# A gate one load later, a copied operand with a place of its own, and a free PSUM bank taken first, in a two-matmul GELU kernel

## The chip, the cores and the metric

The kernel runs on 1 core of one Trainium2 chip. The metric is device time of one execution in microseconds (us); the profile's span is some 1.8 us shorter, because it runs from the first to the last instruction. Most executions agree within 0.3%. Every verdict uses fast runs alone. A ratio is the mean time of one kernel's fast runs over that of the other's of the same rounds, so it is not quite the ratio of the medians quoted beside it. Profiles are one execution each, which will matter below.

## The reference, cut to what matters

```python
m, k, n, p = 1024, 1024, 2048, 1024          # a: m x k, b: k x n, c: n x p, all float32
h = np.matmul(a, b)
h = 0.5 * h * (1 + np.tanh(np.sqrt(2 / np.pi) * (h + 0.044715 * h ** 3)))
return np.matmul(h, c).astype(np.float32)
```

## The kernel before

Both matmuls use a Winograd-like scheme: seven products of quarter matrices instead of eight, paid for with sums of operands on VectorE (`s1` to `s4`, `t1` to `t4`) and with copies on ScalarE (`plain_s`, `plain_t`). The scheme runs three times: `zero` and `one` are parts of the first matmul, `two` is the second.

Twelve plain loads of 512 KB bring `a` and a quarter of `b` as float32. Fourteen casting loads, issued by GpSimd, bring the rest as bf16. A tiny GpSimd copy, the gate, keeps the casting loads back: it reads one element of a plain load, so it waits for that load, and the casting loads stand behind it in GpSimd's queue.

```python
    load_a(0, 0); load_b(0); load_a(1, 0)              # (the kernel has one call a line)
    for q in range(1, 4):
        load_a(0, q)                                   # q = 3: the tenth load
        load_b(q)                                      #        the eleventh
        load_a(1, q)                                   #        the twelfth
    nc.gpsimd.tensor_copy(gate, sta[1][:, 0, 1, 3, 0:1])   # waits for the tenth
    ...
    for _ in range(7):                                 # TensorE warm-up
        nc.tensor.matmul(wps, warm[:, 0:128], warm, start=True, stop=True)
    for k in range(0, KT, 4):                          # the first two casting loads
        nc.gpsimd.dma_start(out=b1[:, k:k + 4, H:], in_=bv[:, k:k + 4, ds(H, H)])
    ...
    def stir(n):                                       # more warm-up, called with 7 and 8
        for _ in range(n):
            nc.tensor.matmul(ps[0, 3][:, 0:128], warm[:, 0:128], warm[:, 0:128],
                             start=True, stop=True, skip_group_check=True)
```

In `one` the operand `s[3]`, a copy that ScalarE makes, shares a buffer (`x01`) with `s[1]`. So it can only be made when product P6 has read `s[1]`, in four pieces during P7. (P1 to P7 are the code's names. In order of running, P5 is the third product, P6 the fourth and P7 the fifth; the "seventh product" of the prediction is P7.)

```python
    one.s = [x31, x01, x21, x01]
    def between1(n):
        ...
        elif n[:2] == "P7":
            one.plain_s(4, int(n[2]))
```

The product loop of `two`, cut. The second product fills PSUM banks 4, 5, 6, which VectorE reads in `plus`; the third product (P5) fills banks 4, 5, 6, 7:

```python
        for j in J if w is not two else range(3):
            p = bank(P2[j])                            # Y = (4, 5, 6, 7)
            w.product(p, A12, B21, j, True)
            done(0, 0, j, plus(p, p1[j]))
        between("P2")
        py = [bank(i) for i in PY]                     # PY = Y as well
        for j in J:
            w.product(py[j], w.s[0], w.t[0], j, True)
```

Of the kernel before, what the change touches and what calls it, by code (L numbers as in the profile page):

```python
# [10 lines left out]
F32R = mybir.dt.float32r  # L11
# [8 lines left out]
def kernel(ctx, tc, a, b, c, out):  # L20
    nc = tc.nc
# [3 lines left out]
    H = 512  # L25
# [14 lines left out]
    def slot(tag, shape, dt, name):  # L40
        return big.tile(shape, dt, name=name, tag=tag)

    def bank(i, shape=(128, H), dt=F32, name="ps"):
        return pp.tile(list(shape), dt, name=name, tag=f"bank{i}", padded_shape=None)

    def pieces(tag, bufs, shape, dt, name):
        return small.tile(shape, dt, name=name, tag=tag, bufs=bufs)
# [5 lines left out]
    gate = consts.tile([128, 1], F32, name="gate")  # L53
# [5 lines left out]
    b1 = slot("b1", [128, KT, 1024], BF16, "b1")  # L59
# [4 lines left out]
    stb = slot("x0", [128, KT, H], F32, "stb")  # L64
    sta = [slot(f"x{i}", [128, 2, 2, 4, 256], F32, "sta") for i in (1, 3)]
# [13 lines left out]
        load_b(q)  # L79
        load_a(1, q)  # L80

    nc.gpsimd.tensor_copy(gate, sta[1][:, 0, 1, 3, 0:1])
    nc.scalar.activation(g, warm[:, 0:1], AF.Gelu_apprx_tanh)
    wps = bank(7, name="warmps")
    for _ in range(7):
# [117 lines left out]
    def quarters(b, c0, w):  # L203
        return [[b[:, 0:4, ds(c0, w)], b[:, 4:8, ds(c0, w)]],
                [b[:, 0:4, ds(c0 + w, w)], b[:, 4:8, ds(c0 + w, w)]]]

    zero = Seven(4, quarters(b1, H, 256), BB, [None] * 4, [None] * 4, 2)
    one = Seven(4, quarters(b2, 0, H), BB, [None] * 4, zero.t)
# [64 lines left out]
    Y = (4, 5, 6, 7)  # L273

    def snap(tag, p, name):
        st = pieces(tag, 4, [128, H], F32, name)
        nc.scalar.activation(st, p, AF.Copy)  # L277
        return st

    def plus(p, st):  # L280
        ot = pieces("o", 4, [128, H], F32, "ot")
        nc.vector.tensor_tensor(out=ot, in0=p, in1=st, op=ADD)  # L282
        return ot

    def seven(w, done, between):

        (A11, A12), (A21, A22) = w.A
        (B11, B12), (B21, B22) = w.B
        J = range(w.n)
        PX = X[:w.n]  # L290
        P2, PY = (X[2:], Y[:2]) if w.n == 2 else (Y, Y)
        px = [bank(i) for i in PX]
        p1, v, u = {}, {}, {}
        for j in J:
            w.product(px[j], A11, B11, j, True)
            if w is two and j == 3:
                p1[j] = pieces("ab", 2, [128, H], F32, "p1")
                nc.scalar.activation(p1[j], px[j], AF.Copy)
            else:
                p1[j] = snap("m", px[j], "p1")  # L300
        between("P1")
        for j in J if w is not two else range(3):
            p = bank(P2[j])
# [3 lines that stand above are left out]
        py = [bank(i) for i in PY]  # L307
        for j in J:
            w.product(py[j], w.s[0], w.t[0], j, True)
        between("P5")  # L310
        for j in J:
            w.product(px[j], w.s[1], w.t[1], j, False)
            v[j] = snap("v", px[j], "v")
        between("P6")
        c22 = []
        for j in J:
            w.product(px[j], w.s[2], w.t[2], j, False)
            u[j] = snap("m", px[j], "u")
            c22.append(plus(py[j], u[j]))
            between(f"P7{j}")  # L320

        def p3(first):
            for j in J:
                if first:
                    done(1, 1, j, c22[j])
                w.product(py[j], w.last_s, w.t[3], j, False)
                done(0, 1, j, plus(py[j], v[j]))
            between("P3")

        def p4(first):  # L330
            for j in J:
                if first:
                    done(1, 1, j, c22[j])
                w.product(px[j], w.s[3], w.last_t, j, False)
                done(1, 0, j, px[j])

        for i, f in enumerate((p4, p3) if w.n == 2 else (p3, p4)):
            f(i == 0)
        if w is two:

            for i in range(2):
                r = ds(i * 256, 256)
                p = bank(Y[i])
                w.product(p, A12, B21, 3, True, i * 256, 256)
                ot = pieces("e", 2, [128, 256], F32, "ot")
                nc.vector.tensor_tensor(out=ot, in0=p[:, r], in1=p1[3][:, r], op=ADD)  # L346
                store(3, i * 256, 256, ot)


    two = Seven(8, [[hT[0][:, 0:8], hT[0][:, 8:16]], [hT[1][:, 0:8], hT[1][:, 8:16]]],  # L350
                [[c_sb[:, 0:8, 0:H], c_sb[:, 0:8, H:]], [c_sb[:, 8:16, 0:H], c_sb[:, 8:16, H:]]],
                [None] * 4, [None] * 4)
# [16 lines left out]
        gelu(8 + 4 * i + j, l, p)  # L369

    def between1(n):
        if n == "P2":
            one.s3()
        elif n == "P5":
            one.s4(one.s[0])
        elif n[:2] == "P7":
            one.plain_s(4, int(n[2]))
        elif n == "P3":
            two.t[0] = slot("x1", [128, 8, H], F32R, "x2")
            two.t1(4)  # L380
            two.s[0] = slot("b2", [128, 8, H], F32R, "s2")
            two.s1(4)
            two.t[1] = slot("x2", [128, 8, H], F32R, "x2")
            two.t2(4)

    zero.s1()
    zero.s2()
    seven(zero, done0, between0)
    one.s1()
    one.s2()  # L390
    seven(one, done1, between1)


# [4 lines left out]
    def store(mt, q0, w, ot, eng=None):  # L398
        (eng or nc.sync).dma_start(out=out[ts(mt, 128), ds(q0, w)], in_=ot)
# [11 lines left out]
    def between2(n):  # L411
# [12 lines left out]
        elif n == "P73":  # L424
            two.t4(two.t[1], 4)

    seven(two, done2, between2)


# [28 lines left out]
```

## Time and profile before

| | before |
|---|---|
| time, median of 4 runs | 121.95 us (121.84 to 122.01) |
| the profiled execution | 122.19 us, span 120.4 us |
| TensorE busy | 112.5 us, 93% of the span |
| VectorE / ScalarE busy | 75% / 48% |

TensorE is the bound, so only its gaps can be won. The lines that show them are in the prediction below. One part of the page I had passed over. It is the list of DMA queues, with packets, MB and the share of sixteen engines' time:

```profile
q0 software_dynamic: 5344, 7.34, 34.9%
q1 hardware_dynamic: 8192, 10.49, 25.5%
q8 instruction: 4, 0.07, 0.2%
q14 instruction: 2, 0.02, 0.0%
```

The first two are the casting and the plain traffic. The `q8` row is four packets of 16 KB, and 0.2% of the DMA time. It turned out to decide the largest term of the prediction.

### The profile page before, as it was taken

To read this page: it belongs to the slowest core of one execution; us is meant where nothing else is said; L and a number is where in the kernel's file an instruction comes from. 1 tells how busy PE (TensorE), PEld (TensorE's weight loads), DVE (VectorE), ACT (ScalarE), POOL (GpSimd) and SP (SyncE) were. 2 spreads that over 40 slices of the span, in tenths; PEclk is the share of its full clock that TensorE was granted. 3 is DMA by queue.
4 is the path that set the end of the run, shared out by engine and by line. 5 is a ranking of instruction groups with operands and counts; after the bars stand their busy time and mean duration, and the time that the engine had idled before them with its cause. 6 is when DMAs were issued, how large, how long until landed. Compare 5 with 4: busy or idle time off the path is not lost.

```text
span 120.4 us, 1483 instructions
## 1 busy us (share of the span) xinstructions
PE 112.5 (93%) x550; PEld 76.0 (63%) x550; DVE 90.1 (75%) x96; ACT 57.9 (48%) x96; POOL 11.0 (9%) x21
## 2 busy tenths in 40 slices
PE   6997999499999999999999999999999999999990
PEld 2644454144677645888887444468888888888860
DVE  0243678389898599970669999999999986964570
ACT  4046343898877584436969736900023893000000
POOL 2000008932242000000000000000000000000000
PEclk9999999999999999999999999999999999999998
DMA  3999999999999999997000000043000002004993
GB/s 97 274 375 361 365 355 275 197 206 207 207 207 211 211 213 212 210 211 148 3 0 0 5 0 0 0 147 115 0 0 0 0 5 87 0 8 181 363 357 137
DMA packets 13542, 17.91 MB, mean 149 GB/s; under 512 B 736, under 2 KB 8928, under 8 KB 13536
## 3 DMA queue, kind: packets, MB, share of 16 engines
q0 software_dynamic: 5344, 7.34, 34.9%
q1 hardware_dynamic: 8192, 10.49, 25.5%
q8 instruction: 4, 0.07, 0.2%
q14 instruction: 2, 0.02, 0.0%
HBM read 20.97 MB, written 4.19 MB: 209 GB/s over the span
## 4 chain that ended last, share of the span: by engine, by line
PE 59%; DVE 10%; SPq 9%; DMA 9%; issue 5%; ACT 5%; ACTq 0%; DVEq 0%
PE ps L193 55%; DMA sta<-in_a_dram 9%; SPq L68 5%; DVE s L151 4%; DVE x L151 4%; SPq L72 4%; PE ps L106 3%; DVE ot L282 2%; ACT u L277 2%; ACT hT L110 1%; ACT x L189 1%; ACT ab L100 1%; PE pt L129 1%; DVE ot L346 0%; ACTq L100 0%
## 5 line engine op out<-in xcount | busy, mean ns | idle before, releaser
L193 PE MATMUL ps<-x,s 128*128 128x512 f32 x128 | 29.5, 390 | 0.1
L193 PEld LDWEIGHTS ps<-x,s 128*128 128x128 f32 x128 | 24.0, 188 | 5.6 <-DVE ot L282 0.6
L193 PE MATMUL ps<-x,x 128*128 128x512 f32 x80 | 19.1, 394 | 0.0
L106 PE MATMUL ps<-aT,b 128*128 128x512 bf16 x64 | 15.9, 379 | 2.4 <-ACT b L135 1.4
L193 PEld LDWEIGHTS ps<-x,x 128*128 128x128 f32 x80 | 15.0, 188 | 3.3
L193 PE MATMUL ps<-x 128*128 128x512 f32 x72 | 16.8, 391 | 0.0
L193 PEld LDWEIGHTS ps<-x 128*128 128x128 f32 x72 | 13.2, 188 | 3.3 <-ACT v L277 0.2
L277 ACT ACTIVATE v<-ps 128x512 f32<-128x512 f32 x10 | 6.0, 598 | 18.3 <-PE ps L193 18.3
L193 PE MATMUL ps<-c_sb,hT 128*128 128x512 bf16 (+1 forms) x72 | 14.2, 355 | 0.2 <-ACT hT L110 0.2
L110 ACT ACTIVATE hT<-ot 128x512 bf16<-128x512 f32 x18 | 10.8, 627 | 4.3 <-DVE ot L282 4.2
L282 DVE TENSOR_TENSOR ot<-ps,v 128x512 f32<-128x512 f32 x10 | 6.7, 688 | 6.7 <-DMA out_dram<-ot 3.9
L106 PEld LDWEIGHTS <-b 128*128 128x128 bf16 x64 | 5.8, 97 | 9.3 <-ACT b L135 2.5
L193 PEld LDWEIGHTS <-hT 128*128 128x128 bf16 x72 | 7.0, 98 | 7.3 <-issue 0.8
L130 DVE COPY aT<-pt 128x1024 bf16<-128x1024 bf16 x8 | 5.5, 692 | 7.3 <-PE pt L129 7.3
L282 DVE TENSOR_TENSOR ot<-ps,u 128x512 f32<-128x512 f32 x10 | 6.8, 691 | 5.7 <-ACT u L277 5.7
L193 PE MATMUL ps<-aT,b 128*128 128x512 bf16 x48 | 10.7, 379 | 0.0
L151 DVE TENSOR_TENSOR x<-c_sb 128x1024 fp32r<-128x1024 bf16 x8 | 9.2, 1216 | 0.0
L193 PEld LDWEIGHTS <-b 128*128 128x128 bf16 x48 | 4.6, 98 | 5.7 <-issue 0.3
L135 ACT ACTIVATE b<-stb 128x512 bf16<-128x512 f32 (+1 forms) x9 | 4.7, 573 | 6.8 <-DMA stb<-in_b_dram 6.8
L110 ACT ACTIVATE hT<-ps 128x512 bf16<-128x512 f32 x14 | 7.3, 601 | 0.1
L277 ACT ACTIVATE p<-ps 128x512 f32<-128x512 f32 x9 | 5.3, 595 | 3.9 <-PE ps L193 3.9
L100 ACT ACTIVATE ab<-sta 128x1024 bf16<-128x1024 f32 x4 | 4.2, 1057 | 5.9 <-DMA sta<-in_a_dram 4.0
(41 smaller groups left out, 114.1 us busy)
## 6 DMA issues: line engine op xcount, KB each, us to landing
sta<-in_a_dram SPq DMA_DIRECT2D x8, 512.0 KB, 9.2
c_sb<-in_c_dram POOLq DMA_DIRECT2D x8, 512.0 KB, 19.8
b<-in_b_dram POOLq DMA_DIRECT2D x6, 512.0 KB, 10.9
out_dram<-ot SPq DMA_DIRECT2D x12, 256.0 KB, 2.1
stb<-in_b_dram SPq DMA_DIRECT2D x4, 512.0 KB, 9.0
out_dram<-ot SPq DMA_DIRECT2D x8, 128.0 KB, 2.0
```

What stands on the lines that cost most here:

```text
L68: nc.sync.dma_start(out=sta[q // 2][:, h, q % 2], in_=av[:, 4 * h:4 * h + 4, ds(q * 256, 256)])
L72: nc.sync.dma_start(out=stb[:, 2 * q:2 * q + 2], in_=bv[:, 2 * q:2 * q + 2, 0:H])
L100: nc.scalar.activation(dst, src, AF.Copy)
L106: nc.tensor.matmul(p, b1[:, k, ts(t, 128)], aT[:, h, k], start=(k == 0), stop=(k == KT - 1))
L110: nc.scalar.activation(hT[h][:, t], p, AF.Gelu_apprx_tanh)
L129: nc.tensor.transpose(pt[:, n, ts(m, 128)], ab[:, m, ts(n, 128)], ident)
L130: nc.vector.tensor_copy(aT[:, h, 2 * q:2 * q + 2], pt)
L135: nc.scalar.activation(b1[:, k, r], stb[:, k, r], AF.Copy)
L151: nc.vector.tensor_tensor(out=dst[:, r], in0=x[:, r], in1=y[:, r], op=op)
L193: nc.tensor.matmul(p[:, ds(c0, w)], l[:, k, ts(j, 128)], r[:, k, ds(c0, w)], start=(start and k == 0), stop=(k == self.kt - 1), skip_group ...
L277: nc.scalar.activation(st, p, AF.Copy)
L282: nc.vector.tensor_tensor(out=ot, in0=p, in1=st, op=ADD)
```

## The change

Its intent: open the gate one load later, so that the last plain loads are not disturbed; make the copy early and in a place of its own, so that ScalarE is free at the end of the first matmul; let the third product of the second matmul start in bank 7, which nobody is reading. The diff without its line numbers:

```diff
-    nc.gpsimd.tensor_copy(gate, sta[1][:, 0, 1, 3, 0:1])
+    nc.gpsimd.tensor_copy(gate, stb[:, 7, 0:1])
 ...
         P2, PY = (X[2:], Y[:2]) if w.n == 2 else (Y, Y)
+        if w is two:
+            PY = (7, 4, 5, 6)
 ...
-                p = bank(Y[i])
+                p = bank(PY[i])
 ...
     def between1(n):
-        if n == "P2":
+        if n == "P1":
+            one.plain_s()
+        elif n == "P2":
             one.s3()
         elif n == "P5":
             one.s4(one.s[0])
-        elif n[:2] == "P7":
-            one.plain_s(4, int(n[2]))
 ...
+    one.s[3] = slot("b1", [128, 2, 4, H], F32R, "x1")[:, 0]
     one.s1()
```

## The prediction

> **What bounds the kernel now.** I read the page's busy shares first, then the waits of TensorE, then the timeline around each of them.
>
> ```profile
> PE 112.5 (93%) x550; PEld 76.0 (63%) x550; DVE 90.1 (75%) x96; ACT 57.9 (48%) x96; POOL 11.0 (9%) x21
> ```
>
> TensorE is busy for 112.5 of 120.4 us. Only 7.9 us of the span are not matmul, so a change that leaves the matmuls alone can at best take idle time out of that. The waits of TensorE say where it lies; one wait stands under the weight loads, since the load comes first:
>
> ```profile
> PE ps L106 <- ACT b L135: 1.4, 2, 1.1
> ...
> PE pt L129 <- ACT ab L100: 0.7, 1, 0.7
> PE ps L193 <- ACT hT L110: 0.2, 1, 0.2
> ...
> PEld ps L193 <- DVE ot L282: 0.6, 1, 0.6
> ```
>
> About 1.2 us (first memset), 0.3 and 0.8 us (first blocks) and some 3.3 us at the end (last matmul at 117.1, span 120.4) are untouched by the change. What it can touch is four gaps: 1.08 us at 20.98, 0.73 us at 23.1, 0.17 us at 66.24 and 0.63 us at 78.15, together 2.61 us. The timeline shows the first two:
>
> ```profile
> 18.45 0.18 POOL L82 COPY gate<-sta 128x1 f32<-128x1 f32 x1 [17.14 <-DMA sta<-in_a_dram]
> 18.57 1.62 POOL L90 DMA_DIRECT2D b<-in_b_dram  x2
> ...
> 21.39 1.15 ACT L135 ACTIVATE b<-stb 128x512 bf16<-128x512 f32 x2 [1.83 <-DMA stb<-in_b_dram]
> ...
> 22.07 1.04 PE L106 MATMUL ps<-aT,b 128*128 128x512 bf16 x4 [1.08 <-ACT b L135]
> 22.73 1.06 ACT L100 ACTIVATE ab<-sta 128x1024 bf16<-128x1024 f32 x1 [0.20 <-DMA sta<-in_a_dram]
> ...
> 23.84 0.62 PE L129 MATMUL pt<-ident,ab 128*128 128x128 bf16 x8 [0.73 <-ACT ab L100]
> ```
>
> The gate opens at 18.45, when the tenth load has landed; the eleventh (b) is there only at 21.37, the twelfth (a) at 22.65. The seven loads between the landings seen at 8.15 and 18.42 came 1.47 us apart; the eleventh took 2.9 us. The bandwidth by half microseconds falls from 377 GB/s (19.0 to 19.5) to 324, 170 and 59 GB/s (20.5 to 21.0) and then rises to the casting loads' steady 207. So the last two plain loads are held up by the casting loads that the gate let in.
>
> The other two gaps:
>
> ```profile
> 65.79 2.04 ACT L110 ACTIVATE hT<-ps 128x512 bf16<-128x512 f32 x4
> ...
> 66.41 12.25 PE L193 MATMUL ps<-c_sb,hT 128*128 128x512 bf16 x56 [0.17 <-ACT hT L110]
> ...
> 73.52 4.62 DVE L151 TENSOR_TENSOR x<-c_sb,x 128x1024 fp32r<-128x1024 bf16 x4
> ...
> 78.06 1.88 DVE L282 TENSOR_TENSOR ot<-ps,p 128x512 f32<-128x512 f32 x3
> ...
> 78.79 6.22 PEld L193 LDWEIGHTS ps<-x,s 128*128 128x128 f32 x28 [0.63 <-DVE ot L282]
> ```
>
> At 66.24 the second matmul wants bank 0, which a GELU still reads. At 78.15 its third product (four groups of eight matmuls) wants bank 4, which the addition of the second product reads only at 78.06 to 78.75, because VectorE does 12 operand sums in one run (64.44 to 78.1) before it.
>
> **What the Trainium skill says.** "DMA: Bandwidth & Descriptors", section "Queues, rings and completion order": each DMA engine takes turns, packet by packet, between the queues that have work. The trace agrees in kind: 2.9 us in place of 1.47 us for the eleventh load. The same page, "Specifications", gives the GpSimd path about 1 us to its first byte; here the bandwidth dips about 1.1 us after the gate. "ScalarE: Activation LUTs", "What ACT_TABLE_LOAD costs": 186 ns + 0.833 ns per element with immediate operands, so 613 ns for 512 and 1892 ns for 2048; the trace has 623 to 660 for 512 and 1047 to 1057 for 1024 (page: 1039). "PSUM — Partial Sum Buffer", "PSUM bank collisions raise a hardware error": an access of another engine must be guarded by bank. That is why bank 4 waits for VectorE; the trace shows it as the 0.63 us.
>
> **Part 1, the gate.** No instruction is added. The gate now waits for the eleventh load, which undisturbed lands at 18.42 + 1.47 = 19.9 (estimate from the spacing); the twelfth at 21.3. First bytes of the casting loads then come about 1.1 us later, at 21.0. By then the plain loads are nearly through: summing bandwidth by time up to 20.0 gives 6.20 of their 6.29 MB (12 x 524,288 bytes). So the eleventh is cast at 19.95 to 21.1, before TensorE wants it at 20.98 with its first half, and the 1.08 us gap closes. ScalarE casts the twelfth at 21.35 to 22.4 and TensorE transposes at 22.5 in place of 23.84: 1.3 us gained there. It is not the full 1.81 us, as TensorE, now done at 21.9, still waits 0.5 to 0.6 us for this load.
>
> What the part costs: the casting loads start 1.45 us later on the queue. They no longer share with the plain loads, so they land later by less. In the kernel before, the first two landed at about 25.24 and 27.77 (read from the descriptor waits of the loads behind them, and 2.53 us apart as all later ones). I put the second at 28.2 to 28.7. The first product of the first matmul's second stage needs the first of them at 28.26 - 1.3 = 27.0: no wait. Its second product comes 1.8 us later, at 28.8: none, just. But VectorE's sums of that stage need the second load. They then run nearly without a break: two sums of 1.24, two additions of 0.65, two sums of 1.14 and t4 in two halves that end 2.36 us later, 8.3 us in all. TensorE wants the second half of t4 at 37.7 now (fourth product, third matmul) and gets it at 37.21, a slack of 0.5 us. With VectorE starting at 28.3 it ends at 36.6, TensorE would want it at 36.4; with 28.8, at 37.1. So of 1.3 us, 0.2 to 0.7 is lost again. Net gain 0.6 to 1.1, middle 0.85 us.
>
> The later casting loads (up to 56 now) have slack: the first that the next stage needs landed by 37.9 and is read at 41.0; c's are first read at 64.44.
>
> **Part 2, the copied operand.** Four ScalarE copies of 0.62 to 0.66 us leave the seventh product of the first matmul's last stage; one copy of 128x2048, about 1.9 us, comes at that stage's first product, at 45.3, where ScalarE next has work at 47.05 and later idles 3.1 us before 52.68. It pushes the GELUs there by 0.2 us, off the path. Around 56 to 60 ScalarE goes u, copy, u, copy; without the copies the fourth u starts 0.3 us earlier and the first GELU at about 59.65 instead of 60.37. The chain of GELU and addition behind it moves 0.7 us relative to TensorE, so bank 0 is free at about 65.7, before TensorE's 66.24: gap 3 goes, 0.17 us. VectorE's run of sums also starts 0.7 us earlier, which is spare.
>
> **Part 3, the bank.** Bank 7 was last read by the addition at 63.83, and the second product doesn't use it. The sums that the third product reads are ready at 68.97 (t) and 73.6 (s). So it starts at once: 0.63 us. Its second group wants bank 4 eight matmuls of 0.23 us later, 1.84 us after the old place, when the addition is done. The later sums (s3, t3) ran 1.3 us ahead of TensorE at the tightest, and this part takes 0.6 of that. Nothing follows.
>
> Sum: 0.85 + 0.17 + 0.63 = 1.65 us; 121.95 - 1.65 = 120.3 us.
>
> **The rivals.** (a) The casting loads come a full 1.5 us later. For: the gate and the descriptor work do move so, and the dip to 59 GB/s looks like a start-up time that is paid anyway. Against: they no longer share with the 0.25 MB of plain loads that were left at 19.6. The second would land at 29.2, t4 would end at 37.6, the gate gains nothing, and the whole is 121.1. (b) The casting loads land where they did, the slowest DMA engine having the same work. Then t4 ends early enough, and the whole is 1.25 + 0.8 = 2.05 us: 119.9. (c) Another wait takes the place of the bank's: VectorE, 100% busy from 66 to 90, could become the bound as TensorE moves up. Against: its run starts 0.7 us earlier too. At worst 0.6 us comes back: 120.9. (d) The plain loads finish still sooner and the 0.73 gap closes as well: all 2.61 us, 119.3. Their spacing of 1.47 us speaks against it.
>
> **Range and chances.** Parts 2 and 3 give 0.5 to 0.8; the gate -0.1 to 1.3. Range 119.8 to 121.1. Over 2% would be 2.44 us, nearly all four gaps: 4%. Slower by 2% needs a wait that I have not seen: 1%. Within 2%: 95%.
>
> **What would show it.** Right: the gate at about 19.9, the twelfth load's cast at 21.3 to 21.5, no wait on ACT b at 21, transposes at 22.5, then a new wait of TensorE on a VectorE sum (x of line 151) at about 36 of some tenths; no waits at the entry of the second matmul's first and third product. Wrong: a wait on the casting load itself at 27 to 29, a cast of the twelfth load still after 22.5, or a new gap at the bank of the third product's second group or at s3/t3.

## The result, and the profile after

The changed kernel takes 121.27 us (121.19 to 121.30, 4 runs), ratio 0.9944 (0.9927 to 0.9961). I had said 120.3, in a range of 119.8 to 121.1. The time is within 2% as forecast, but the gain is 0.68 us where 1.65 was forecast, and the time lies outside the range.

The waits of TensorE in the changed kernel (us in total, times, longest):

```profile
PE pt L129 <- ACT ab L100: 1.5, 1, 1.5
PE warmps L86 <- DVE warm L50: 1.2, 1, 1.2
PE ps L106 <- DVE aT L130: 0.8, 1, 0.8
PE ps L106 <- ACT b L135: 0.4, 1, 0.4
```

The waits at the second matmul (on ACT hT, on DVE ot) are gone. The wait for the eleventh load (ACT b) has shrunk to the 0.4 us that belongs to the first block. But the wait for the twelfth (ACT ab) has grown from 0.7 to 1.5 us. The timeline at that place (start us, us, engine, line, operation, and in brackets the idle time before it and its releaser):

```profile
19.90 1.15 ACT L135 ACTIVATE b<-stb 128x512 bf16<-128x512 f32 x2 [0.22 <-DMA stb<-in_b_dram]
19.93 0.39 POOL L82 COPY gate<-stb 128x1 f32<-128x1 f32 x1 [18.62 <-DMA stb<-in_b_dram]
...
20.25 1.62 POOL L90 DMA_DIRECT2D b<-in_b_dram  x2
...
22.61 1.06 ACT L100 ACTIVATE ab<-sta 128x1024 bf16<-128x1024 f32 x1 [1.56 <-DMA sta<-in_a_dram]
...
23.72 0.62 PE L129 MATMUL pt<-ident,ab 128*128 128x128 bf16 x8 [1.47 <-ACT ab L100]
```

The eleventh load came at 19.9 and the gate opened there, both as predicted. The twelfth did not come at 21.3. Its cast starts at 22.61, against 22.73 before, so the transposes moved from 23.84 to 23.72: 0.12 us for a term that I had put at 0.85. The wait only moved from one load to the next.

Two more readings need the trace's records beneath these views. The trace keeps when each of a load's sixteen shares (one for each DMA engine) is reported as landed, and when each packet starts:

```
before:  eleventh load  15 shares 18.92 to 19.75, the 16th 21.36
         twelfth load   15 shares 20.37 to 21.15, the 16th 22.63
after:   eleventh load  16 shares 19.09 to 19.87
         twelfth load   15 shares 20.55 to 21.27, the 16th 22.51
first casting packet: before 20.16, after 21.85
instruction packet of 16 KB on q8: before 19.19 for 1.12 us, after 19.34 for 1.14 us
```

One share of sixteen is late by 1.2 us and more, so one DMA engine was busy with something else. In the changed kernel it was no casting load: the first casting packet starts at 21.85, and from 20.5 to 22.05 the plain queue moves only 9 to 11 KB in each half microsecond. All sixteen engines moved about 184 KB in a half before that, and a sixteenth of it is 11.5 KB, so this looks like one engine alone, catching up. (The records of packets don't name their engine.) What came just before is a 16 KB packet of the instruction queue, which took 1.14 us.

The page "Runtime: NRT & Kernel Launch" of the Trainium skill, section "Instruction fetch mechanics", says that each engine's instructions are refilled in 16 KiB blocks of 256 instructions. The trace is in keeping with that. The four packets of `q8` in the kernel before start when 215, 439, 661 and 909 of TensorE's weight loads and matmuls have started, thus every 222 to 248 of them. (Semaphore instructions between them are not in this count.)

The timeline of the changed kernel at the entry of the second matmul:

```profile
63.57 4.62 DVE L151 TENSOR_TENSOR x<-c_sb 128x1024 fp32r<-128x1024 bf16 x4
64.92 2.04 ACT L110 ACTIVATE hT<-ps 128x512 bf16<-128x512 f32 x4
...
65.95 12.26 PE L193 MATMUL ps<-c_sb,hT 128*128 128x512 bf16 x54
...
77.19 1.88 DVE L282 TENSOR_TENSOR ot<-ps,p 128x512 f32<-128x512 f32 x3
...
77.86 22.14 PE L193 MATMUL ps<-x,s 128*128 128x512 f32 x96
```

The GELUs that free bank 0 start at 64.92 instead of 65.79. The first product starts at 65.95 instead of 66.41, 0.34 us more than the shift of 0.12 that was there. From its start to that of the third product it is 77.86 - 65.95 = 11.91 us, against 78.79 - 66.41 = 12.38 before, so 0.47 us less. VectorE's sums start 0.87 us earlier (63.57 against 64.44), and the additions behind them at 77.19 instead of 78.06.

The chain of waits that ended last, by engine, before and then after:

```profile
PE 59%; DVE 10%; SPq 9%; DMA 9%; issue 5%; ACT 5%; ACTq 0%; DVEq 0%
```

```profile
PE 77%; SPq 9%; DMA 9%; ACT 1%; issue 1%; DVE 0%; ACTq 0%
```

ScalarE and VectorE have gone from the chain after the twelfth load's cast. What is left ahead of TensorE's work is the plain loads (SPq and DMA, 18%), which end with the straggling share.

Adding up the traces gives 0.12 + 0.34 + 0.47 = 0.93 us, but the medians differ by only 0.68. The profiled execution of the kernel before took 122.19 us, 0.24 above its median. It is also the one profile with the old warm-up in which the eleventh load had a late share, as shown above.

### The profile page after: what moved, and what is told of

The parts are those of the page before. It is cut to its first block, busy times and chain, and to the rows that moved or that the text cites. A ratio compares the mean times of both kernels' runs of the same rounds, so it can differ in the third digit from the quotient of the medians.

```text
span 119.5 us, 1474 instructions
## 1 busy us (share of the span) xinstructions
PE 111.5 (93%) x544; PEld 75.6 (63%) x550; DVE 90.1 (75%) x96; ACT 57.9 (48%) x93; POOL 11.2 (9%) x21
## 4 chain that ended last, share of the span: by engine, by line
PE 77%; SPq 9%; DMA 9%; ACT 1%; issue 1%; DVE 0%; ACTq 0%
PE ps L193 73%; DMA sta<-in_a_dram 9%; SPq L68 6%; SPq L72 4%; PE ps L106 3%; ACT ab L100 1%; PE pt L129 1%; DVE ot L348 0%; ACTq L100 0%
## 5 line engine op out<-in xcount | busy, mean ns | idle before, releaser
L193 PE MATMUL ps<-x,x 128*128 128x512 f32 x96 | 22.8, 393 | 0.0
L193 PEld LDWEIGHTS ps<-x,x 128*128 128x128 f32 x96 | 18.0, 188 | 3.9
L193 PE MATMUL ps<-x 128*128 128x512 f32 x56 | 13.2, 392 | 0.0
L193 PEld LDWEIGHTS ps<-x 128*128 128x128 f32 x56 | 10.2, 188 | 2.6 <-ACT u L277 0.4
L277 ACT ACTIVATE u<-ps 128x512 f32<-128x512 f32 x10 | 5.9, 597 | 3.4 <-PE ps L193 3.2
```

The costliest lines, as they stand in the source:

```text
L193: nc.tensor.matmul(p[:, ds(c0, w)], l[:, k, ts(j, 128)], r[:, k, ds(c0, w)], start=(start and k == 0), stop=(k == self.kt - 1), skip_group ...
L277: nc.scalar.activation(st, p, AF.Copy)
```

## The experiments

Three questions: what is each part worth alone, is the fetch the cause of the late share, and what is the gate worth when the fetch is out of the way. The runs were made in three calls, each on another chip and with its own runs of the kernel before (medians 122.00, 121.89 and 122.01). So runs of different calls are compared by their ratios to these.

### Each part alone

`gate_only`: the first line of the diff alone.

```diff
-    nc.gpsimd.tensor_copy(gate, sta[1][:, 0, 1, 3, 0:1])
+    nc.gpsimd.tensor_copy(gate, stb[:, 7, 0:1])
```

> The kernel before with the gate at the eleventh load, nothing else. My first theory (on record: casting loads hold up the last two plain loads) expects the twelfth load's cast at about 21.4 us and 0.85 us less in all: 121.1. The new theory (a 16 KB fetch of TensorE's instructions, seen in both traces at 19.2 to 19.3 us for 1.1 us, holds up one DMA engine and so one sixteenth of the last load) expects the cast at 22.5 to 22.6 as in the changed kernel, and 0.1 us less or nothing: 121.8 to 121.95.

Measured: 121.97 us (13 runs) against 122.00, ratio 0.9999 (0.9991 to 1.0007). The last share of the twelfth load landed at 22.48, and the fetch came at 19.35. The gate is worth nothing here. The cast of the twelfth load:

```profile
22.58 1.06 ACT L100 ACTIVATE ab<-sta 128x1024 bf16<-128x1024 f32 x1 [1.53 <-DMA sta<-in_a_dram]
```

`operand_only`: the copied operand in its own place.

```diff
-        if n == "P2":
+        if n == "P1":
+            one.plain_s()
+        elif n == "P2":
             one.s3()
         elif n == "P5":
             one.s4(one.s[0])
-        elif n[:2] == "P7":
-            one.plain_s(4, int(n[2]))
 ...
+    one.s[3] = slot("b1", [128, 2, 4, H], F32R, "x1")[:, 0]
```

> The kernel before with the copied operand in its own place, nothing else. The two traces have the second matmul's start 0.46 us earlier, of which 0.12 was there before it: so 0.34 us less, 121.6. The prediction had 0.17 us, from the length of the gap that the profile names. No change would mean that the bank wait later eats it up (it should not: VectorE moves up as well).

Measured: 121.28 us, ratio 0.9942 (0.9930 to 0.9955): 0.72 us less. That is the whole gain of the change, and twice what I expected. Its timeline tells why:

```profile
65.89 12.26 PE L193 MATMUL ps<-c_sb,hT 128*128 128x512 bf16 x56
...
77.13 1.87 DVE L282 TENSOR_TENSOR ot<-ps,p 128x512 f32<-128x512 f32 x3
77.86 4.19 PEld L193 LDWEIGHTS ps<-x,s 128*128 128x128 f32 x19 [0.21 <-DVE ot L282]
77.87 4.39 PE L193 MATMUL ps<-x,s 128*128 128x512 f32 x18
```

The idle time at the bank is down from 0.63 to 0.21 us although the banks are the old ones. From the first product's start to the third's it is 77.87 - 65.89 = 11.98 us, against 12.38 before: 0.40 us less. VectorE's run of sums starts earlier, so the addition that frees bank 4 comes earlier as well.

`bank_only`: the new order of banks.

```diff
+        if w is two:
+            PY = (7, 4, 5, 6)
 ...
-                p = bank(Y[i])
+                p = bank(PY[i])
```

> The kernel before with the third product's banks 7, 4, 5, 6, nothing else. Prediction: 0.63 us less, 121.3. From the two traces (start of the third product 0.93 us earlier, 0.46 of it there already) 0.47 us: 121.5.

Measured: 121.61 us, ratio 0.9967 (0.9955 to 0.9979): 0.39 us less. The distance from the first to the third product's start is 78.25 - 66.35 = 11.90 us, almost as in the changed kernel (11.91):

```profile
66.35 12.25 PE L193 MATMUL ps<-c_sb,hT 128*128 128x512 bf16 x56 [0.17 <-ACT hT L110]
...
78.25 4.01 PE L193 MATMUL ps<-x,s 128*128 128x512 f32 x16
```

`operand_bank`: both, with the gate as it was.

> The kernel before with the copied operand and the banks, gate as it was. The operand alone gave 0.72 us, the banks alone 0.39, the whole change 0.68. If the operand already moves VectorE's run far enough to take most of the bank's wait with it, both together give 0.75 to 0.85 (in the trace of the operand alone 0.2 us of the bank's wait were left): 121.2. If the two add up and the gate costs what is missing, 0.72 + 0.39 = 1.11: 120.9.

Measured: 121.33 us, ratio 0.9945 (0.9932 to 0.9959). Neither expectation was quite right. The two together give what the operand gives alone (121.28), so within the noise the bank adds nothing once the operand is moved, and the gate does not take back a gain of theirs either. They share one wait.

### The instruction fetch

`after_wide`: the changed kernel with 22 TensorE instructions fewer before the loads end, for about the same TensorE time.

```diff
-            nc.tensor.matmul(ps[0, 3][:, 0:128], warm[:, 0:128], warm[:, 0:128],
+            nc.tensor.matmul(ps[0, 3], warm[:, 0:128], warm,
 ...
-    stir(7)
+    stir(2)
 ...
-    stir(8)
+    stir(2)
```

> The changed kernel with its 15 warm-up matmuls of 128 columns replaced by 4 of 512: the same TensorE time within 0.2 us, 22 TensorE instructions fewer before the loads end. Theory of the instruction fetch: the fetch comes some 22 instructions later, at 20.4 to 21 us, when the plain loads' bytes are all moved; all sixteen shares of the twelfth load land by 21.4, its cast starts at 21.4 instead of 22.6, the transposes at 22.5 instead of 23.7; of the 1.2 us some 0.9 reach the end because VectorE's sums then wait for the second casting load (28.3): 120.4. Theory of the casting loads' traffic: nothing changes, cast at 22.6, 121.27.

Measured: 120.62 us, ratio 0.9886 (0.9872 to 0.9899) to the kernel before. The fetch starts at 20.49, the last share of the twelfth load lands at 21.24, and the timeline has:

```profile
21.35 1.06 ACT L100 ACTIVATE ab<-sta 128x1024 bf16<-128x1024 f32 x1 [0.34 <-DMA sta<-in_a_dram]
...
22.46 0.62 PE L129 MATMUL pt<-ident,ab 128*128 128x128 bf16 x8 [0.25 <-ACT ab L100]
...
28.48 1.23 DVE L151 TENSOR_TENSOR x<-b 128x1024 fp32r<-128x1024 bf16 x1 [1.27 <-ACT hT L110]
...
36.81 3.05 PEld L193 LDWEIGHTS ps<-x 128*128 128x128 f32 x14 [0.25 <-DVE x L151]
```

This is what I had predicted for the change itself, down to the transposes at 22.5. So is the price that I had named: VectorE's sums stand idle for 1.27 us until 28.48 (the second casting load's last share landed at 28.30; the releaser in the bracket is not the one that came last), and TensorE waits for one of them at 36.8.

`after_wide_padded`: the same, with as many tiny matmuls added at the start as were removed.

```diff
+    for _ in range(11):
+        nc.tensor.matmul(wps[:, 0:16], warm[:, 0:128], warm[:, 0:16], start=True, stop=True)
```

> The faster variant (4 wide warm-up matmuls in place of 15 narrow ones) with 11 matmuls of 16 columns added right at the start: as many TensorE instructions before the loads end as the changed kernel has. Theory of the instruction fetch: the fetch is back at 19.3, the last share of the twelfth load at 22.5, and the time at 121.27 or slightly under. If instead the wide warm-up matmuls themselves brought the 0.65 us (a warmer TensorE, say), it stays at 120.6.

Measured: 121.04 us, ratio 0.9932 (0.9920 to 0.9945). The fetch is back at 19.35, the last share of the twelfth load lands at 22.51, and TensorE waits as in the changed kernel (its line numbers are two higher):

```profile
PE pt L131 <- ACT ab L102: 1.4, 1, 1.4
```

So it was the number of instructions, not the wide warm-up. Its median is 0.2 us under the changed kernel's, and the intervals overlap; I leave that open.

`after_narrow`: the changed kernel with 42 TensorE instructions more at the start.

```diff
-    for _ in range(7):
-        nc.tensor.matmul(wps, warm[:, 0:128], warm, start=True, stop=True)
+    for _ in range(28):
+        nc.tensor.matmul(wps[:, 0:128], warm[:, 0:128], warm[:, 0:128], start=True, stop=True)
```

> The changed kernel with its 7 first warm-up matmuls of 512 columns cut into 28 of 128: 42 TensorE instructions more at the start. Theory of the instruction fetch: the fetch comes at 16 to 17.5 us, in the middle of the loads; from then on one share of each load is up to 1.1 us late: the tenth load at 19.6, the eleventh and with it the gate at 21.0 instead of 19.9, the twelfth at 22.5 as before. The second casting load lands about 1 us later (29.4), and its sums hold TensorE up: 121.3 to 121.8, middle 121.55. Theory of the casting traffic: warm-up instructions don't matter, 121.27, tenth load at 18.5.

Measured: 121.55 us (121.20 to 121.80), ratio 0.9963 (0.9950 to 0.9976). The fetch starts at 17.63, somewhat later than I expected. The late share now begins with the tenth load (fifteen by 18.60, the last at 19.91), goes on with the eleventh (21.23) and ends with the twelfth (22.64):

```profile
20.02 1.06 ACT L100 ACTIVATE ab<-sta 128x1024 bf16<-128x1024 f32 x1 [3.23 <-DMA sta<-in_a_dram]
21.13 0.62 PE L129 MATMUL pt<-ident,ab 128*128 128x128 bf16 x8 [1.02 <-ACT ab L100]
```

The gate opened at 21.28 and the second casting load landed at 29.51, as expected. The delay goes where the fetch goes. The delayed share stays behind for the plain loads that follow. (The first casting load's last share, at 27.02, is only 0.13 us behind its fifteenth.)

`before_wide`: the wide warm-up alone, on the kernel before.

> The kernel before with only the 4 wide warm-up matmuls in place of the 15 narrow ones: the instruction fetch is moved and nothing else of the change is there. Theory of the instruction fetch: all shares of the twelfth load by 21.2, transposes at 22.4, about 1.2 us less as in the run with the gate at the tenth load (120.01 against some 121.2 for operand and banks alone): 120.8. If the gain needs the change's other parts, 121.5 or more.

Measured: 120.82 us, ratio 0.9906 (0.9893 to 0.9920), as the fetch theory expected. Three lines of warm-up, with nothing of the change, gain 1.19 us: more than the whole change. Its profile fell in a slow run (122.72 us), so no trace shows the fetch and the loads of its fast runs, and the time can't be explained from it. But that trace holds a warning. One share of sixteen is late there too, by 0.6 us at the second load and by about 1.0 us from the third to the twelfth, which is whole only at 22.43; the first 16 KB fetch starts at 20.85. So a late share by itself does not name the fetch as its cause; what named it here is that the share moved with the fetch in `after_wide`, `after_wide_padded` and `after_narrow`. What delayed it in the slow run stays open.

### The gate

`after_gate12`: the changed kernel with the gate at the twelfth load.

```diff
-    nc.gpsimd.tensor_copy(gate, stb[:, 7, 0:1])
+    nc.gpsimd.tensor_copy(gate, sta[1][:, 1, 1, 3, 0:1])
```

> The changed kernel with the gate at the twelfth load: no casting load can share with any plain load. Theory of the instruction fetch: fifteen shares of the twelfth load land by 21.3 and the last at 22.5 all the same, its cast starts at 22.6, the transposes at 23.7; the casting loads come 2.6 us later still, the second at 30.9 instead of 28.3, so VectorE's sums end later and TensorE waits: 2 to 2.5 us slower than the changed kernel, 123.5. Theory of the casting traffic: the twelfth load lands whole at 21.3 and its cast starts at 21.4; the loss by the later casting loads is smaller, about 1.3 us: 122.5.

Measured: 123.04 us, ratio 1.0099 (1.0083 to 1.0116). The time fell between the two expectations, but the trace decides:

```profile
22.36 1.06 ACT L100 ACTIVATE ab<-sta 128x1024 bf16<-128x1024 f32 x1 [1.68 <-DMA sta<-in_a_dram]
...
30.59 1.90 PE L193 MATMUL ps<-aT,b 128*128 128x512 bf16 x8 [0.60 <-DMA b<-in_b_dram]
```

No casting packet starts before 24.0, and still fifteen shares of the twelfth load land by 20.90 and the sixteenth at 22.25. The fetch starts at 18.89 here. The second casting load lands at 30.55, and TensorE now waits for it: a cost that a gate can have.

`rest_wide_gate10`: wide warm-up, operand and banks of the change, and the gate at the tenth load again.

```diff
-    nc.gpsimd.tensor_copy(gate, stb[:, 7, 0:1])
+    nc.gpsimd.tensor_copy(gate, sta[1][:, 0, 1, 3, 0:1])
```

> The faster variant with the gate back at the tenth load: what the gate is worth when no instruction fetch disturbs. If casting loads do share with the last two plain loads and hold them up (my theory on record), the eleventh or the twelfth lands later than 19.9 and 21.3, by 0.5 us or more, and the time is 121.0 or more. If they hardly do (first casting bytes at 19.9 to 20.0, when 6.2 of 6.29 MB are moved), the twelfth lands by 21.6, the second casting load at 27.3 instead of 28.3, so the sums behind it no longer hold TensorE up, and the time is 120.2 to 120.5.

Measured: 120.01 us (119.87 to 120.30), ratio 0.9849 (0.9834 to 0.9864) to the kernel before. It beats both kernels. The twelfth load lands whole at 21.10, no later than with the later gate (21.24), and VectorE's sums start 1.2 us earlier than in `after_wide`, with 0.19 us of idle time before them instead of 1.27:

```profile
21.20 1.06 ACT L100 ACTIVATE ab<-sta 128x1024 bf16<-128x1024 f32 x1 [0.34 <-DMA sta<-in_a_dram]
...
27.25 1.23 DVE L151 TENSOR_TENSOR x<-b 128x1024 fp32r<-128x1024 bf16 x1 [0.19 <-issue]
```

So with the fetch out of the way the later gate costs about 0.5 us (ratios 0.9886 and 0.9849, each to the kernel before of its own call) and protects nothing.

`wide_gate9`: the same with the gate at the ninth load.

```diff
-    nc.gpsimd.tensor_copy(gate, sta[1][:, 0, 1, 3, 0:1])
+    nc.gpsimd.tensor_copy(gate, sta[1][:, 1, 0, 3, 0:1])
```

> The fastest variant so far (120.01) with the gate one load earlier still, at the ninth. First casting bytes then come at about 18.5, when 0.6 MB of plain loads are still to move. If sharing costs the plain loads what the prediction thought, the twelfth load lands 0.5 to 1.3 us later than 21.1 and the time is 120.5 to 121.3. If they lose less than 0.3 us, 120.0 to 120.3; there is nothing to gain, since no wait on VectorE's sums is left there.

Measured: 120.14 us, ratio 0.9847 (0.9832 to 0.9862): the same as with the tenth. Of the casting packets 152 start before 21 us, and the twelfth load still lands whole at 21.06. The gate opened a load earlier, but the first casting packet came only 0.3 us earlier (19.77 against 20.08), and 59 packets had started before 21 us with the gate at the tenth load. At this size of overlap the sharing that I feared cannot be seen. How much overlap would hurt I have not tried.

## Why the prediction was wrong

**The gate (0.85 us predicted, 0 measured).** The step that failed is "So the last two plain loads are held up by the casting loads that the gate let in". The runs showed that TensorE's instruction fetch holds them up. It occupied one DMA engine for 1.1 us and made one share of sixteen late, whether casting packets were there (before), came later (after) or were kept away altogether (`after_gate12`).

My own numbers spoke against the step. I had summed up 6.20 of 6.29 MB as moved by 20.0, and took the fall in bandwidth from there on for the casting loads pushing in. It was the plain loads running out. The first casting packet of the kernel before started at 20.16, 1.6 us after its issue. The 2.9 us that I set beside the skill's turn-taking between queues was one late share: the other fifteen of the eleventh load had landed by 19.75.

The second mistake in this term was to take one profile for the kernel. The 1.08 us gap at the eleventh load belongs to that execution, in which the fetch started at 19.19. In the profiles of `operand_only`, `bank_only` and `operand_bank`, which have the old gate as well, the fetch started at 19.34 to 19.36 and the eleventh load landed whole by 19.84 to 19.92. So most of what I meant to win there was not to be won. Why that one execution lost a share of the eleventh load stays open: in `after_gate12` the fetch came earlier still, at 18.89, and the eleventh was whole at 19.51.

The rest of the term was right where it could be tested. The second casting load landed at 28.34 (I had said 28.2 to 28.7), and when the twelfth load did come at 21.24, the transposes started at 22.46 and TensorE met VectorE's late sum, as predicted for 36 and some tenths. (The run of sums took 8.27 us in `after_wide`, from 28.48 to 36.75, where I had said 8.3; the terms that I listed add up to 8.4.) In `gate_only` the later landing is free, because TensorE and VectorE are late themselves: the sums start at 28.46 in any case.

**The copied operand (0.17 us predicted, 0.72 alone).** The mechanism was right up to the start of VectorE's run: the first GELU at 59.44 (predicted 59.65), the wait at bank 0 gone, and VectorE's run 0.75 us earlier after the shift of 0.12 is taken off (predicted 0.7). ScalarE's single copy took 1.90 us, where the formula of the Trainium skill's "ScalarE: Activation LUTs", section "What ACT_TABLE_LOAD costs", gives 1.89. Two things were wrong. The gap was mis-sized: the first product starts 0.34 us earlier where the profile's idle time says 0.17. And the step "VectorE's run of sums also starts 0.7 us earlier, which is spare" failed. That run ends in the addition that frees bank 4, so the 0.7 us go straight into the wait that part 3 was to remove, and take away 0.40 of its 0.47 us (by the starts of the products).

**The bank (0.63 us predicted, 0.39 alone, nothing on top of the operand).** The mechanism was right: the third product starts at once. The size was read from a row of the weight loads. Its 0.63 us contains a pause of 0.12 us that the weight loads of the second product have before them with no gap of the matmuls at all; the starts of the products say 0.47. And the step "Sum: 0.85 + 0.17 + 0.63" added two parts that remove the same wait. Together they give 0.68 us (`operand_bank`), where 0.72 + 0.39 would be 1.11. I had also put the wait at bank 4 down to the skill's rule on banks. By the code the third product overwrites there what VectorE has yet to read, so it would have to wait without that rule; no run here tests the rule.

**The range.** It doesn't follow from its own parts. Gains of 0.5 to 0.8 us and -0.1 to 1.3 us add up to 0.4 to 2.1 us, so to 119.85 to 121.55; the range ended at 121.1. A gate worth nothing, as measured, was within the part given for it.

**The rivals.** Rival (a) named 121.1, nearest to the result, but by a second casting load at 29.2, which did not come. No rival had the right cause. Rival (c), VectorE as the new bound, did not appear.

## What to carry to other kernels

A load is there when its slowest share is there, so look at the spread of the shares before blaming other loads: fifteen on time and one late points at a single DMA engine, though not yet at what keeps it busy. Two parts of a change that sit on the same chain of one engine are not added; ask for each "spare" shift which wait stands at the end of that engine's run. Before a gap of a microsecond carries a forecast, compare it with a second execution, and measure gaps of matmuls between their starts: at the bank the idle time of the weight loads said 0.63 us and the starts 0.47.

## What the Trainium skill lacked or had wrong

- "Runtime: NRT & Kernel Launch", "Instruction fetch mechanics", calls the cost of crossing a 16 KiB boundary mostly hidden. No wait of TensorE's matmuls is put down to a fetch here, but the fetch runs on a DMA engine that also carries loads, which the page doesn't say. It took 1.12 to 1.16 us there while the plain loads ran and made one share of a load some 1.2 us late. With 22 TensorE instructions fewer before the loads end, the kernel before took 1.19 us less (120.82 against 122.01); when as many were put back in the changed kernel, all but some 0.2 us of its gain was gone. The number of instructions moved the fetch: it started at 20.49 with 22 fewer and at 17.63 with 42 more, against 19.34.
- "DMA: Bandwidth & Descriptors", "Specifications", has about 1 us to the first byte on the GpSimd path. Here it was 1.6 us from the start of the issue to the first casting packet (18.57 to 20.16, and 20.25 to 21.85), and 2.3 us in `wide_gate9` (17.48 to 19.77).
- The same page, "Queues, rings and completion order", has the engines take turns between queues. It gives no size for what a load loses by it; here, with 152 casting packets started before 21 us, the twelfth load landed at 21.06, against 21.24 with none.
